# Two-layer hybrid encoder on one Trainium2 core: the modulation groups laid out anew, and the opening reordered

## The chip, the cores and the metric

The kernel runs on one core of one Trainium2 chip. The metric is the device time of one execution in microseconds (us), given as the median of several runs. Beside the runs there is one profiled execution, whose trace is the source of every duration below. Engines are named as the profile names them: PE is TensorE (matmuls; PEld its weight loads), DVE is VectorE, ACT is ScalarE, POOL is GpSimd, SP is SyncE, which here does nothing but issue DMAs.

## The reference, cut to what matters

A trunk of two layers over x of 1024 tokens by 1024 channels, all in float32, with one condition vector c. Each layer first turns c into six modulation vectors of 1024 numbers:

```
cond = silu(c)
for l in range(2):
    mod = cond @ w_mod[l] + b_mod[l]                  # 1 x 6144
    sh_a, sc_a, gt_a, sh_f, sc_f, gt_f = split(mod, 6)  # groups 0..5 of the layer
    h = rms_norm(x, g_attn[l]) * (1 + sc_a) + sh_a
    y = three_head_groups(h @ w_in[l])                # A, B and C, each with its own RMSNorm
    x = x + gt_a * (y @ w_o[l])
    h = rms_norm(x, g_ffn[l]) * (1 + sc_f) + sh_f
    gate, up = split(h @ w_gu[l], 2)                  # 1024 -> 2 x 2816
    x = x + gt_f * ((silu(gate) * up) @ w_down[l])    # 2816 -> 1024
return rms_norm(x, g_final)
```

A group is one of these six vectors of one layer, written (layer, group): (0,5) is gt_f of the first layer, (1,0) is sh_a of the second. Each needs a 1024 x 1024 block of w_mod, 4 MB, read once.

## The kernel before

x is kept transposed, channels on partitions, in eight chunks of 128 channels by 1024 tokens. A product of float32 accuracy is made of three fp32r matmuls: both operands are split into a high and a low part, and `mm3` adds high x high, low x high and high x low. ACT makes the high part (a cast), DVE or POOL the low one (a subtraction), into the `wpt` or `whl` buffers. Gate/up and down are Strassen-like: seven products instead of eight per block, with sums of weights made by DVE ahead.

**The stages and the engines' order.** In the opening, in the projections of the attention stage and in some others the instructions of an engine are pinned to the order of the source; elsewhere a scheduler in the compiler chooses the order by readiness. SP is pinned through gate/up and down. Whatever order results, each engine runs its own instructions one after the other, and SP its DMA issues.

**Opening.** Groups (0,0) and (0,1) come first, because h of layer 0 needs them. They are made in four pairs p, each of two channel chunks, from eight half loads `gm` of 1 MB: `gemv_half(i)` adds three weighted rows on DVE and lets PE add the rest into one row of PSUM; after the second half of a pair ACT copies the row to `gr`. `gemv_turn(p)` turns it into columns (four small PE transposes), `gemv_finish(p)` adds the bias on DVE, and `h_blocks(half, rows, ns)` makes the chunks ns of h for one half of the tokens: DVE scales (`nt`), ACT writes the high part `hh`, DVE the low part `hl`. `pair_done(p)` is the three of them in a row for the first half. `c_first(n)` then multiplies chunk n of that half with the weights of head group C, 12 matmuls into four banks `pssC`. The second half of x is squared (`x_square`), its norm is taken (`x_rms`, `spread` to rows) and it is transposed (`x_turn`) in between. After the opening, the loop over t goes on with `c_proj(4, 5)`, the same projection for the first two 128-token blocks of the second half, 48 matmuls over chunks 0 to 7.

**Modulation groups beside the matmuls.** The other groups run beside the main work, in the order of the list `todo`: (0,2) to (0,5), then (1,0) to (1,5). In each layer's attention stage `mod_one` takes 24 steps, three whole groups. In gate/up, `mod_stream(psl, shared, until)` is a generator: each `next` issues the load `wmt` of the next half row block (128 x 512, 256 KB) on SP and lets DVE add the block loaded before, weighted by c, to the accumulator `acc`; 16 such adds make a group. Then `mod_parts` and `mod_flush` split `acc` in two halves and sum each over the partitions: two matmuls on PE (`ps_mod`), and a cast, two multiplications or subtractions and a reduction on DVE. With all pauses a group takes 24 calls of `next`. The tiles of the loads come from a tag that `shared` names, `sq` with two buffers in gate/up.

**Gate/up.** There are 22 column blocks q. The first seven run two products early; then each q from 7 on runs seven products of 12 matmuls. For each product ACT copies (`take`) or DVE adds the result out of its bank before a later product may write it; the operands are prepared by `ahead.fill()` on ACT, DVE and POOL. The kernel before calls `next(mods_due)` after each product from q = 7 (`EARLY`) on, until (1,3): in layer 0 that is the four groups (0,5), (1,0), (1,1) and (1,2); in layer 1 the list is empty by then.

**Down.** 77 units u of 12 matmuls, prepared four units ahead: two high and two low parts per unit, `graw` loads of two units at a time from DRAM. After every eleventh unit DVE adds the banks into x (`residual`). After unit 54 of layer 0 the squares and h of layer 1 begin beside it, for which (1,0) and (1,1) must be there.

Of the kernel before, what the change touches and what calls it, by code (L numbers as in the profile page):

```python
# [19 lines left out]
P = 128  # L20
# [65 lines left out]
def trunk(ctx: ExitStack, tc, A, C, out):  # L86
# [266 lines left out]
    def mod_stream(psp, shared, until):  # L353


        pl, tag, bufs, width = shared
        acc = None
        while todo and todo[0] < until:
            l, g = todo[0]
            first = going["step"]  # L360
            if first == 0:
                going["acc"] = cp.tile([P, 1024], F32, name="acc", tag="acc")
            acc = going["acc"]
            halves = [(k, c0) for k in range(first, KC) for c0 in range(0, 1024, width)]
            loads = {}

            def load(i):
                k, c0 = halves[i]
                st = loads[i] = pl.tile([P, width], F32, name="wmt", tag=tag, bufs=bufs)
                g0 = g * 1024 + c0  # L370
                sp.dma_start(st, A["w_mod"][l, k * P : (k + 1) * P, g0 : g0 + width])

            if halves:
                load(0)
                yield
            for i, (k, c0) in enumerate(halves):
                if i + 1 < len(halves):
                    load(i + 1)
                mod_add(k, acc[:, c0 : c0 + width], loads.pop(i))
                yield  # L380
            going["step"] = KC
            mod_parts(slice(0, width), shared)
            while going["step"]:
                yield
                yield
                yield
                mod_flush(psp)
            yield
# [56 lines left out]
    def spread(r, j0, psp, tag="mm"):  # L445

        ps = psp.tile([P, 512], F32, name="ps_r", tag=tag)
        for j in range(4):
            pe.transpose(
                ps[:, j * P : (j + 1) * P], bc(r[:, j0 + j : j0 + j + 1], [P, P]), ident  # L450
            )
        return ps
# [116 lines left out]
    def x_rms(r):  # L569
        act.activation(r, r, AF.Sqrt, bias=epst, scale=1.0 / D)  # L570
        dve.reciprocal(r, r)

    def x_turn(half, xn, ns, engines):

        c = slice(half * H, (half + 1) * H)
        for n in ns:
            ps = psl.tile([P, 512], F32, name="ps_x", tag="mm")
            for i in range(4):
                pe.transpose(
                    ps[:, i * P : (i + 1) * P], xn[i][:, n * P : (n + 1) * P], ident  # L580
                )
            if engines[n % 2] is act:
                act.copy(xt[:, n, c], ps)
            else:
                dve.tensor_copy(xt[:, n, c], ps)
# [23 lines left out]
            rows = A["w_mod"][0, r0 : r0 + 4 * P, c0 : c0 + 2 * P]  # L609
            sp.dma_start(gm[:, :, g, :], rows.rearrange("(k p) n -> p k n", p=P))  # L610

    def gemv_half(i):
        p, s = i // 2, i % 2
        gm = gms.pop(i).rearrange("p k g n -> p k (g n)")
        if s == 0:
            gas[p] = stp.tile([P, 4 * P], F32, name="ga", tag="ga", bufs=2)
            gps[p] = psl.tile([P, 4 * P], F32, name="ps_mod", tag="mm")
        ga, row = gas[p], gps[p][0:1]
        for k in range(3):
            mod_add(4 * s + k, ga, gm[:, k])  # L620
        pe.matmul(row, condT[:, 4 * s + 3 : 4 * s + 4], gm[:, 3], start=(s == 0), stop=False)
        if s:
            pe.matmul(row, ones, ga, start=False, stop=True)
            gas[p] = stp.tile([1, 4 * P], F32, name="gr", tag="gr", bufs=1)
            act.copy(gas[p], row)

    def gemv_turn(p):

        ps = gps[p] = psl.tile([P, 4], F32, name="ps_m", tag="mm")
        row = gas.pop(p)  # L630
        for c in range(4):
            pe.transpose(ps[:, c : c + 1], row[:, c * P : (c + 1) * P], ident[0:1, 0:1])
# [35 lines left out]
            sp.dma_start(dst, v)  # L668
        wcs.append(st)

    def c_first(n):

        wh, wl = wC[n // 2]
        for t in range(T0):
            ts_ = slice(t * P, (t + 1) * P)
            mm3(
                pssC[t], hh[:, n, ts_], hl[:, n, ts_], wh[:, n % 2], wl[:, n % 2],
                n == 0, n == KC - 1,
            )
# [52 lines left out]
    def pair_done(p):  # L732
        gemv_turn(p)
        gemv_finish(p)
        if p == 0:
            keep_busy(8)
        h_blocks(0, rb, (2 * p, 2 * p + 1))
# [39 lines left out]
    pair_done(2)  # L777
    x_square(1, 1, xns[1][1], rxs[1])
    c_first(4)
    c_first(5)  # L780
    w_split()
    wab.append(w_ab(0, 1))
    spill(0)
    gemv_half(7)
    pair_done(3)
    for j in (2, 3):
        x_square(1, j, xns[1][j], rxs[1])
    x_rms(rxs[1])
    x_turn(1, xns[1], range(4), (act, act))
    c_first(6)  # L790
    x_turn(1, xns[1], range(4, KC), (act, act))
    c_first(7)
    spill(1)
    rows = spread(rxs[1], 0, psl)
    turn_vecs(1, v1)
    gm = stp.tile([P, 2048], F32, name="gm", tag="gm", bufs=3)
    first_t1 = c_norm_first(pssC[0], gm[:, 0:512], gm[:, 512:1024], gm[:, 1024:1032])
    for n in range(0, KC, 2):
        h_blocks(1, rows, (n, n + 1))
    sp.dma_start(sinkc, bc(A["sink_sw"].rearrange("l h -> (l h)")[None, :], [P, 12]))  # L800
    for l in range(2):
# [9 lines left out]
    for l in range(2):  # L811
# [1166 lines left out]
            shifted_sub(b21, b21, shift(2 * i + 1), t2)  # L1978
            h_split("t4", i, b21, dve)

        mods_due = mod_stream(psl, (ntp, "sq", 2, H), (1, 3))
        bs = []
        rows = None
        norm = rstd_rows(ssq, ntp, psl)
# [24 lines left out]
        for q in range(NF):  # L2009
            if q % 2 == 0:  # L2010
                gu_start(q // 2)
            if q == NF - 1:
                pin([act], True)
            if q < EARLY:
                up = q % 2
                e = sg[q // 2][0][:, 0:H]
                if up:
                    pool.tensor_tensor(out=e, in0=e, in1=quads[q]["11"], op=ALU.mult)
            for i, p in enumerate(PRODUCTS[2 if q < EARLY else 0 :]):
                gu_product(q, p, ahead.get())  # L2020
                if i == 1 and q < EARLY and not up:
                    act.activation(e, quads[q]["11"], AF.Silu)
                ahead.fill()
                g_step()
                if q >= EARLY:
                    next(mods_due, None)
        for _ in mods_due:
            pass
# [164 lines left out]
                yield  # L2193

        beside = iter(())
        for u in range(NU):
            i, t = divmod(u, NB)
            num, _, bank = DOWN[i]
            for what in due.get(u, ()):
                what()  # L2200
            ahead.fill(4)
            if u % 2 == 0 and (u + 6) // 2 <= (NU - 1) // 2:
                b_load((u + 6) // 2)
            for _ in range(3 if steps else 0):
                g_step()
            if u == 5:
                xt = blocks(xp)
            if t == 0 and num == 2:
                acc_b = [psl.tile([P, 512], F32, name="ps_d", tag="mm") for _ in range(4)]
            banks = acc_a if bank == "a" else acc_b  # L2210
            a, b = ahead.have.pop(0)
            for j in range(4):
                js = slice(j * P, (j + 1) * P)
                mm3(
                    banks[j], a[:, 0, js], a[:, 1, js], b[:, 0], b[:, 1],
                    num in (1, 2, 5) and t == 0, t == NB - 1, skip_group_check=True,
                )
            next(beside, None)
            if u >= NU - 2 and not last_layer:
                if u == NU - 2:  # L2220
                    wC = []
                wC.append(split_w(w_in_src(1, C_COLS, len(wC)), 2, eng=dve))
            if t < NB - 1:
                continue
            m, half = {
                1: (0, 0), 2: (0, 0), 6: (0, 1), 7: (1, 1), 4: (1, 0), 5: (1, 1), 3: (0, 1),
            }[num]
            for j in range(4):
                residual(banks[j], 2 * j + m, slice(half * H, half * H + H), 40)
            if num == 4:  # L2230
                close(w2_cm)
                close(w1_cm)
                if last_layer:
                    fn_cm, fnp = open_pool("fin", side="right")
                    gf = fnp.tile([P, D], F32, name="gf")
                    sp.dma_start(gf, bc(A["g_final"][None, :], [P, D]))
                else:
                    h_cm, hp = open_pool("h", side="right")
                    hh = hp.tile([P, KC, S], F32R, name="hh")
                    hl = hp.tile([P, KC, S], F32R, name="hl")  # L2240
                    cc_cm, ccp = open_pool("cc", side="right")
                    csts.clear()
                    g8 = gains_load(ccp, 1)
                    for n in range(KC):
                        at_unit(57 + 2 * n, lambda n=n: spill(0, [n]))
                beside = chain(early_half(), odd_squares())
# [111 lines left out]
```

## Time and profile before

| | |
|---|---|
| median of 3 runs | 2448.36 us (2446.49 to 2448.49) |
| the profiled execution: its own time | 2449.54 us |
| its span, first to last instruction | 2447.8 us |
| mean granted TensorE clock | 0.994 |
| instructions | 34293 |
| busy: PE, DVE, ACT, POOL | 97%, 74%, 50%, 31% of the span |
| DMA, mean over the span | 145 GB/s |

The page's busy shares are unions of an engine's instructions over the whole span. The view of windows gives the same for chosen stretches, with the granted clock (1.00 is full speed). The view of waits sums up how long an engine sat idle before a kind of instruction, and the instruction or DMA that ended it. In the views a line such as `ps_w<-ht3h,wpt` is an instruction that writes tile ps_w from ht3h and wpt; all lines are those of one helper (L49), so tiles tell them apart. `ps_w` are the banks of gate/up, `ps_d` of down, `ps_c` of the C projection.

### The profile page before, as it was taken

To read this page: it belongs to the slowest core of one execution; us is meant where nothing else is said; L and a number is where in the kernel's file an instruction comes from. 1 tells how busy PE (TensorE), PEld (TensorE's weight loads), DVE (VectorE), ACT (ScalarE), POOL (GpSimd) and SP (SyncE) were. 2 spreads that over 40 slices of the span, in tenths; PEclk is the share of its full clock that TensorE was granted. 3 is DMA by queue.
4 is the path that set the end of the run, shared out by engine and by line. 5 is a ranking of instruction groups with operands and counts; after the bars stand their busy time and mean duration, and the time that the engine had idled before them with its cause. 6 is when DMAs were issued, how large, how long until landed. Compare 5 with 4: busy or idle time off the path is not lost.

```text
span 2447.8 us, 34293 instructions
## 1 busy us (share of the span) xinstructions
PE 2385.3 (97%) x12005; PEld 1991.1 (81%) x12005; DVE 1819.0 (74%) x2968; ACT 1224.3 (50%) x2306; POOL 768.3 (31%) x783
## 2 busy tenths in 40 slices
PE   8999999999999999999999999999999999999998
PEld 5788899878788787788888889987887888888886
DVE  6757999987967777587677689998698555446865
ACT  3422888954543333334543158888454343334443
POOL 1531445620344343300036124464005434430001
PEclk9999999999999999999999999999999999999999
DMA  8468205154245453596434851241634432239743
GB/s 284 152 188 289 56 11 145 49 180 147 87 153 178 149 182 123 166 278 200 142 104 120 262 181 27 64 133 51 206 93 136 136 106 95 99 104 285 216 135 109
DMA packets 284181, 356.04 MB, mean 145 GB/s; under 512 B 32996, under 2 KB 201532, under 8 KB 284008
## 3 DMA queue, kind: packets, MB, share of 16 engines
q1 hardware_dynamic: 275512, 335.08, 44.1%
q10 hardware_dynamic: 6912, 12.59, 1.6%
q0 software_dynamic: 1584, 6.17, 0.7%
q8 instruction: 95, 1.56, 0.3%
q14 instruction: 78, 0.64, 0.1%
HBM read 269.62 MB, written 86.69 MB: 146 GB/s over the span
## 4 chain that ended last, share of the span: by engine, by line
PE 71%; DVE 11%; DMA 6%; issue 5%; ACT 4%; POOL 1%; SPq 1%; ACTq 0%; POOLq 0%; DVEq 0%
PE ps_w L49 28%; PE ps_d L49 10%; PE ps_o L49 7%; PE pv L49 6%; PE ps_ab L49 6%; PE T L49 4%; PE sC L49 3%; PE ps_c L49 2%; PE ps_v L49 2%; DMA wmt<-in_w_mod_dram 2%; DVE wpt L49 2%; DMA w<-in_w_down_dram 2%; ACT pr L49 1%; PE sA L49 1%; DVE w L49 1%
## 5 line engine op out<-in xcount | busy, mean ns | idle before, releaser
L49 PE MATMUL ps_d<-wpt 128*128 128x512 f32 x1848 | 425.2, 391 | 2.1 <-DVE wpt L49 0.9
L49 PEld LDWEIGHTS ps_d<-wpt 128*128 128x128 f32 x1848 | 345.6, 188 | 77.0 <-DVE wpt L49 3.1
L49 POOL TENSOR_SCALAR pr<-pr,rs 128x1024 f32<-128x1024 f32 (+4 forms) x252 | 206.9, 823 | 271.6 <-DVE rs L49 254.9
L49 POOL TENSOR_TENSOR sg<-sg,u 128x512 f32<-128x512 f32 x86 | 123.5, 1437 | 359.4 <-ACT sg L49 227.9
L49 PE MATMUL pv<-pt,vs 128*128 128x256 f32 x1216 | 202.1, 297 | 7.9 <-DVE rs L49 2.3
L49 DVE TENSOR_TENSOR pt<-T,pt 128x512 fp32r<-128x512 f32 x304 | 199.6, 681 | 11.4 <-ACT pt L49 9.9
L49 ACT CAST pt<-T 128x512 fp32r<-128x512 f32 x304 | 170.0, 586 | 43.8 <-PE T L49 41.9
L49 PE MATMUL T<-identr,pr 128*128 128x128 f32 x1288 | 187.1, 273 | 2.2 <-ACT rb L49 1.0
L49 ACT COPY u<-ps_w 128x512 f32<-128x512 f32 x128 | 75.2, 587 | 214.8 <-PE ps_w L49 214.8
L49 PEld LDWEIGHTS pv<-pt,vs 128*128 128x128 f32 x1216 | 161.3, 190 | 22.9 <-DVE y L49 7.6
L49 DVE TENSOR_TENSOR wpt<-w,wpt 128x512 fp32r<-128x512 f32 x154 | 111.6, 725 | 83.7 <-ACT wpt L49 83.7
L49 PEld LDWEIGHTS T<-identr,pr 128*128 128x128 f32 x1288 | 152.6, 140 | 21.9 <-issue 3.2
L49 POOL TENSOR_TENSOR wpt<-ws,wpt 128x512 fp32r<-128x512 f32 x80 | 112.0, 1401 | 182.8 <-ACT wpt L49 140.6
L49 DVE SCALAR_TENSOR_TENSOR acc<-wmt,condT,acc 128x512 f32<-128x512 f32 (+1 forms) x98 | 112.5, 1158 | 66.2 <-DMA wmt<-in_w_mod_dram 65.6
L49 ACT CAST wpt<-w 128x512 fp32r<-128x512 f32 x154 | 95.5, 620 | 131.3 <-PE ps_d L49 124.1
L49 ACT CAST wpt<-ws 128x512 fp32r<-128x512 f32 x176 | 107.9, 622 | 56.3 <-issue 22.5
L49 ACT CAST wpt<-graw 128x512 fp32r<-128x512 f32 x154 | 95.1, 617 | 78.0 <-DMA graw<-gpd 73.1
L49 DVE TENSOR_TENSOR wpt<-ws,wpt 128x512 fp32r<-128x512 f32 x96 | 83.0, 874 | 57.2 <-ACT wpt L49 57.1
L49 DVE TENSOR_REDUCE rs<-sC 128x1 f32<-128x1024 f32 x96 | 116.5, 1219 | 6.4 <-PE sC L49 6.0
L49 DVE TENSOR_TENSOR ws<-wr 128x512 f32<-128x512 f32 x88 | 82.2, 935 | 52.5 <-POOL wpt L49 49.5
L49 DVE TENSOR_TENSOR wpt<-graw,wpt 128x512 fp32r<-128x512 f32 x154 | 110.9, 720 | 12.5 <-ACT wpt L49 12.5
L49 PE MATMUL ps_w<-ht3h,wpt 128*128 128x512 f32 x352 | 112.0, 400 | 6.9 <-ACT sg L49 6.9
(288 smaller groups left out, 6030.5 us busy)
## 6 DMA issues: line engine op xcount, KB each, us to landing
wr<-in_w_gu_dram SPq DMA_DIRECT2D x92, 512.0 KB, 4.2
gpd<-sg SPq DMA_DIRECT2D x154, 256.0 KB, 4.5
graw<-gpd SPq DMA_DIRECT2D x76, 512.0 KB, 3.8
w<-in_w_down_dram SPq DMA_DIRECT2D x110, 256.0 KB, 5.1
wmt<-in_w_mod_dram SPq DMA_DIRECT2D x48, 512.0 KB, 6.6
qk<-qkd SPq DMA_DIRECT2D x44, 512.0 KB, 7.1
wst<-in_w_o_dram SPq DMA_DIRECT2D x32, 512.0 KB, 3.4
wmt<-in_w_mod_dram SPq DMA_DIRECT2D x64, 256.0 KB, 3.4
```

Of the source, the lines that this page charges most:

```text
L49: ins = op(*args, **kwargs)
```

## The change

Gate/up now calls `next(mods_due)` only after the products i = 0, 2, 4 and 6 of a q, and goes to (l + 1, 1 - l): in layer 0 the two groups (0,5) and (1,0), in layer 1 whatever is left. Down has a stream of its own, one call per unit from u = 37 on, with loads in the three `nt` buffers: in layer 0 that is (1,1), in layer 1 none. The attention stage of layer 1 with its 24 steps then makes (1,2), (1,3) and (1,4) where it made (1,3), (1,4) and (1,5), and gate/up of layer 1 makes (1,5). In all the same twelve groups are made.

In the opening, the last half of the gemv moves ahead of `c_first(5)`; the copy of its row becomes a function of its own (`gemv_row`), issued on ACT after the squares; `c_first(5)` is cut in two around `gemv_turn(3)`; the rows of the second half's norm are spread before `c_first(6)` instead of after `c_first(7)`, and chunks 0 to 3 of the second half's h are issued before `turn_vecs` and `c_norm_first` instead of after them.

```diff
-    def gemv_half(i):
+    def gemv_half(i, copy=True):
...
         if s:
             pe.matmul(row, ones, ga, start=False, stop=True)
-            gas[p] = stp.tile([1, 4 * P], F32, name="gr", tag="gr", bufs=1)
-            act.copy(gas[p], row)
+            if copy:
+                gemv_row(p)
+
+    def gemv_row(p):
+        row = gps[p][0:1]
+        gas[p] = stp.tile([1, 4 * P], F32, name="gr", tag="gr", bufs=1)
+        act.copy(gas[p], row)
...
-    def c_first(n):
+    def c_first(n, ts=None):
...
-        for t in range(T0):
+        for t in ts or range(T0):
...
     c_first(4)
-    c_first(5)
+    gemv_half(7, copy=False)
     w_split()
     wab.append(w_ab(0, 1))
     spill(0)
-    gemv_half(7)
-    pair_done(3)
     for j in (2, 3):
         x_square(1, j, xns[1][j], rxs[1])
     x_rms(rxs[1])
+    gemv_row(3)
+    c_first(5, (0, 1))
+    gemv_turn(3)
+    c_first(5, (2, 3))
+    gemv_finish(3)
+    h_blocks(0, rb, (6, 7))
     x_turn(1, xns[1], range(4), (act, act))
+    rows = spread(rxs[1], 0, psl)
     c_first(6)
+    h_blocks(1, rows, (0, 1))
     x_turn(1, xns[1], range(4, KC), (act, act))
     c_first(7)
     spill(1)
-    rows = spread(rxs[1], 0, psl)
+    h_blocks(1, rows, (2, 3))
     turn_vecs(1, v1)
...
     first_t1 = c_norm_first(pssC[0], gm[:, 0:512], gm[:, 512:1024], gm[:, 1024:1032])
-    for n in range(0, KC, 2):
+    for n in (4, 6):
         h_blocks(1, rows, (n, n + 1))
...
-        mods_due = mod_stream(psl, (ntp, "sq", 2, H), (1, 3))
+        mods_due = mod_stream(psl, (ntp, "sq", 2, H), (l + 1, 1 - l))
...
-                if q >= EARLY:
+                if q >= EARLY and i % 2 == 0:
                     next(mods_due, None)
...
         beside = iter(())
+        mods_due = mod_stream(psl, (ntp, "nt", 3, H), (l + 1, 2))
         for u in range(NU):
             i, t = divmod(u, NB)
+            if u > 36:
+                next(mods_due, None)
             num, _, bank = DOWN[i]
```

## The prediction

> **What bounds the kernel now.** I read the page's first part, then the waits of PE, then windows of the stages that the change touches, and only then the queues behind them.
>
> ```profile
> PE 2385.3 (97%) x12005; PEld 1991.1 (81%) x12005; DVE 1819.0 (74%) x2968; ACT 1224.3 (50%) x2306; POOL 768.3 (31%) x783
> ```
>
> PE works 97% of the span and the change takes no matmul away, so only two things can be won: time in which PE waits, and time in which it runs at a lower clock. The waits of PE, the three longest over the whole span:
>
> ```profile
> PE ps_w L49 <- ACT sg L49: 10.1, 6, 3.0
> PE ps_c L49 <- ACT hh L49: 9.0, 4, 4.4
> PE ps_w L49 <- ACT u L49: 4.2, 5, 1.9
> ```
>
> The first and third are gate/up: PE waits for ACT to copy a bank. The second is the opening. Both are stages that the change touches. Gate/up runs twice, and in layer 1 without modulation, which makes layer 1 the measure. Windows from q = 7 to the last product, layer 0 and layer 1, then down of layer 0 (columns: PE, PEld, DVE, ACT, POOL, clock, DMA share, GB/s):
>
> ```profile
> 730.40:1036.40 306.00, 296.37 (x1278) 242.12 (x1277) 220.44 (x271) 108.80 (x195) 126.30 (x87) 0.98 0.49 159
> 1931.20:2216.80 285.60, 285.60 (x1261) 236.59 (x1260) 137.36 (x170) 110.30 (x195) 117.23 (x87) 1.00 0.34 112
> 1036.40:1250.60 214.20, 212.58 (x938) 174.40 (x937) 161.17 (x250) 98.84 (x171) 13.32 (x10) 1.00 0.66 196
> ```
>
> The same 1260 matmuls take 306.0 us in layer 0 and 285.6 in layer 1, where PE never waits. A matmul is worth 285.6 / 1260 = 0.227 us, a product of 12 is 2.72 us. The 16 `ps_mod` matmuls of four groups are 3.6 us, so 20.4 - 3.6 = 16.8 us are lost in layer 0. PE's waits in that window are 9.6 of them:
>
> ```profile
> PE ps_w L49 <- ACT sg L49: 6.9, 4, 3.0
> PE ps_w L49 <- ACT u L49: 2.7, 3, 1.9
> ```
>
> The other 7.2 are matmuls at a lower clock behind the long waits. A wait and what follows it, twice:
>
> ```profile
> 919.90:922.90 3.00, 0.03 (x2) 0.00 (x1) 3.00 (x6) 1.16 (x3) 0.00 (x0) 0.85 0.11 37
> 922.90:929.30 6.40, 6.40 (x16) 5.06 (x17) 4.25 (x6) 2.29 (x5) 1.50 (x2) 0.54 0.01 1
> 852.80:855.10 2.30, 0.42 (x2) 0.00 (x1) 0.78 (x2) 2.09 (x5) 0.34 (x1) 1.00 0.08 19
> 855.10:859.00 3.90, 3.83 (x17) 3.15 (x18) 2.06 (x3) 1.82 (x5) 3.65 (x3) 1.00 0.97 329
> ```
>
> After 3.0 us without a matmul the clock is 0.54 for 6.4 us, which costs 6.4 x 0.46 = 2.9 us more; after 1.9 us nothing follows. [...]
>
> Why ACT is late in layer 0: not by its own work (108.8 against 110.3 us busy) but because its casts wait for DVE's sums, and DVE stands before a modulation add until its load has landed.
>
> ```profile
> DVE acc L49 <- DMA wmt<-in_w_mod_dram: 47.2, 25, 5.3
> SPq L49 <- DVE wpt L49: 73.5, 10, 16.7
> DMA to landing us min/median/max: 2.6/4.5/8.6
> 730.40:1036.40 306.00, 84.37 (x96) 0.98 0.49 159
> ```
>
> The rows: DVE's wait for `wmt`; SP's own wait for buffers, behind which the `wmt` loads queue; their time to landing; DVE's work on `acc` for four groups, 21.1 us each. A load is issued one step ahead, 2.72 us, and lands after 4.5. So DVE was taken for 220.4 + 47.2 = 268 of 306 us (87%) in layer 0 and 137.4 of 285.6 (48%) in layer 1.
>
> **The change, part by part: gate/up of layer 0.** Two groups go out. Those left are stepped after four products of seven: mostly 5.44 us apart, longer than the 4.5 of a landing, so most of DVE's waits go with it. DVE comes to 137.4 + 42.2 = 180 of 287 us, 63%. Bounds of what stays lost: nothing (layer 1's row) and 8.4 (two groups at 16.8 / 4 each). A straight line from 48% (0) to 87% (16.8) gives 6.5, but a queue that is late now and then holds PE only when the lateness outlasts the 2.72 us of the product in between; I take 2.
>
> **Gate/up of layer 1.** It receives (1,5) at the same pace: 137.4 + 21.1 = 158 us, 55%. Bounds 0 and 4.2; I take 1. The `ps_mod` matmuls only move from stage to stage: 0.9 us a group wherever it runs, nothing in the sum. The attention stage of layer 1 keeps its 24 steps, with other columns of w_mod: nothing.
>
> **Down of layer 0.** Here the new stream runs at one step per unit, 2.72 us, from u = 37 to 60. The window of these units, DVE's wait in it, and the landing of the `graw` loads of down:
>
> ```profile
> 1139.00:1202.00 63.00, 62.92 (x278) 51.87 (x277) 38.52 (x60) 29.45 (x52) 1.00 (x1) 1.00 0.45 134
> L49 DVE TENSOR_TENSOR wpt<-w,wpt 128x512 fp32r<-128x512 f32 x23 | 15.9, 691 | 23.5 <-ACT wpt L49 23.4
> DMA to landing us min/median/max: 3.4/3.8/11.0
> L49 DVE SCALAR_TENSOR_TENSOR acc<-wmt,condT,acc x56: 736/752/1850, 738.8 to 991.6; 128x512 f32<-128x512 f32 x56
> ```
>
> DVE has 24.5 us free of 63. Sixteen adds at 0.75 are 12 (the 1850 ns of the row are adds beside POOL, which is idle here), the two sums some 5: 55.5 of 63, 88%, before any wait for a load. On SP each second `wmt` stands behind the `graw` load of that pair of units, which waits for DVE's last subtraction on its buffer; so the chain subtraction, issue, landing, add, two subtractions must close once in two units. By rows: 0.3 + L + 0.7 + 2 x 0.69 = L + 2.4 us, against 5.44. With L = 4.2 (a `graw` landing and a little, the `wmt` being next behind it) that is 1.2 late per pair, 9 over eight pairs, of which the four units prepared ahead absorb some 6. Bounds: 0 (the scheduler is free to put the add behind the subtractions, DVE not being pinned there) and 9 (nothing absorbed); I take 3. If DVE is late, `residual` after unit 43 is late next, and unit 44 writes the same banks. The three `nt` buffers hold loads two steps old, and x is written to `nt` by `h_chunk` only from unit 65 on: no conflict, nothing. SP's `x_back` and `spill` behind the new loads have many units of lead: nothing, unless SP is late with `graw`, which is the chain just priced.
>
> **The opening.** The rows of PE there (the 49.71 and 74.79 are from the chain of waits: start, length), the windows around the longest pause and behind it:
>
> ```profile
> 57.74 0.40 PE L49 MATMUL ps_m<-identr,gr 1*128 1x1 f32 x4 [0.72 <-ACT gr L49]
> 60.92 0.51 PE L49 MATMUL ps_c<-whi,hl 128*128 128x512 f32 x1 [0.28 <-DVE hl L49]
> 68.97 0.23 PE L49 MATMUL pst<-identr,v 72*128 72x72 f32 x1
> 73.61 0.80 PE L49 MATMUL ps_c<-whi,hh 128*128 128x512 f32 x1 [4.41 <-ACT hh L49]
> 49.71 5.51 PE ps_c L49 x23
> 74.79 12.87 PE ps_c L49 x47
> 68.90:73.60 4.70, 0.30 (x4) 0.11 (x1) 3.82 (x9) 1.06 (x3) 1.37 (x2) 0.84 0.82 251
> 73.60:79.10 5.50, 5.11 (x12) 3.65 (x13) 5.36 (x7) 2.00 (x3) 3.33 (x3) 0.52 0.58 202
> 84.00:135.00 51.00, 51.00 (x268) 42.32 (x266) 43.85 (x67) 21.96 (x50) 34.90 (x29) 1.00 0.42 117
> ```
>
> PE is idle 4.4 us before `c_proj(4, 5)` because chunk 0 of the second half comes only after `turn_vecs` and DVE's five operations of `c_norm_first`; then it runs 5.5 us at 0.52, 5.5 x 0.48 = 2.6 lost, with short waits on `hl` 3.0. I laid the new order out by durations of DVE and ACT:
>
> ```profile
> L49 SPq DMA_DIRECT2D gm<-in_w_mod_dram x16: 367/530/1842, 3.0 to 34.8; - x16
> DMA to landing us min/median/max: 4.6/8.5/10.1
> 52.69 2.32 DVE L49 SCALAR_TENSOR_TENSOR ga<-gm,condT,ga 128x512 f32<-128x512 f32 x3
> 58.58 1.41 DVE L49 SCALAR_TENSOR_TENSOR nt<-xt,vecs,rb 128x512 f32<-128x512 f32 x2
> 59.36 1.38 ACT L49 ACTIVATE hh<-nt,vecs 128x512 fp32r<-128x512 f32 x2 [1.68 <-DVE nt L49]
> 60.12 1.41 DVE L49 SCALAR_TENSOR_TENSOR hl<-nt,vecs,hh 128x512 fp32r<-128x512 f32 x2
> 63.22 3.98 ACT L49 COPY xt<-ps_x 128x512 f32<-128x512 f32 x8
> 72.06 1.40 DVE L49 SCALAR_TENSOR_TENSOR nt<-xt,vecs,ps_r 128x512 f32<-128x512 f32 x2
> ```
>
> `c_first(4)`, the first half of the 24 matmuls to 55.2, ends at about 52.4 as before; the gemv's three adds on DVE, now ahead of the split of the weights, run from 50.3 to 52.7 (the last `gm` load is issued at 34.8 and lands within 10.1). The row is copied on ACT while six matmuls of `c_first(5)` run, and chunks 6 and 7 are made while PE transposes: the 0.7 before the turn, the 0.8 around 60.9 and half a microsecond of small gaps go, 2.0 together, and `turn_vecs` ends near 67.1 instead of 69.2. A pair of chunks takes 1.41 `nt` and 1.41 `hl` on DVE, with `hh` beside. Once the rows are spread (59.6), chunks 0 and 1 are done by 62.6, and 2 and 3, behind four copies of 0.5 on ACT, by 66.6: `c_proj(4, 5)` starts at once. From the end of `turn_vecs` to the next `nt` DVE needs 2.8 as before (69.2 to 72.06), so chunks 4 and 5 start at 69.9: the first is wanted at 67.1 + 24 x 0.227 = 72.5 and has its high part at 71.4; 6 is wanted at 75.2, at 74.3. It ends at 67.1 + 48 x 0.227 = 78.0 instead of 87.7: 9.5 us = 2.0 + 4.5 (idle) + 3.0 (clock). Behind it PE has not waited once from 84 to 135, with DVE 86% busy; DVE is earlier by about 9 and keeps up. The rows `ps_r` hold one more bank for longer, three stay for `x_turn`: some 0.1. On SP `spill` and `w_ab` only start with the work they follow: nothing. Bounds 6 (the two last pairs each late by a wait) and 10.
>
> **Sum**, against the profiled execution: 2449.5 - 9.5 - 16.8 + 2 + 1 + 3 = 2429.2. The median of the runs is 1.2 under the profiled one: 2428.
>
> **The rivals.** (a) The loss belongs to each group, not to its pace: 4.2 us a group wherever it is put, because each group's sums and adds come in clusters. For it: the seven waits of gate/up lie over all four groups. Against: loads that come in time. Then only the opening is won: 2448.4 - 9.5 = 2439. (b) Down: the chain above is late by 9, and one wait at unit 44 reaches 3 us, so the clock falls for 2.9: 8 to 9 in place of 3, 2434. For it: 88%; against: PE waits there now for 0.7 us only, twice. (c) The opening's gain is half given back because DVE, 86% busy behind it, is what really sets the pace: 2433. (d) The other side: the landing of `wmt` in down decides. Without down 23.3 us are won (9.5 + 16.8 - 3); the loss there is 8 x (L + 2.4 - 5.44) - 6, which reaches 23.3 at L = 6.7 us. The longest landing of this tile is 8.6, which gives 38 us and 2463. Against: `graw`, in the same stage, lands in 3.8 by the median. (e) Nothing is won: the waits move elsewhere one for one, and `hh` is late at its later chunks as it was at the first: 2448.
>
> ```profile
> PE ps_d L49 <- ACT wpt L49: 0.7, 1, 0.7
> PE ps_d L49 <- DVE wpt L49: 0.7, 1, 0.7
> ```
>
> (The waits of PE in down of layer 0, for b.)
>
> **How the numbers follow.** The forecast 0.54, (a) 0.12, (b) 0.13, (c) 0.12, (d) 0.05, (e) 0.04. The forecast's own range is 2423 to 2434: all of the 26.3 won and a little from the opening's upper bound, or 6 more lost. The range to 2440 takes in (a), (b) and (c), and leaves out (d) and (e); below, 2420. Faster by over 0.2%, 4.9 us, is the forecast with (a), (b), (c): 0.91; within 0.2%, about what a measurement of this kernel can tell from no change: 0.04; slower: 0.05.
>
> **What would show it.** In the profile after: the wait of 4.41 on `hh` gone and the clock 1.00 where it was 0.52; `c_proj(4, 5)` ending near 78; gate/up of layer 0 from q = 7 in 288 to 291 us and of layer 1 in 286 to 289; DVE's wait for `wmt` there well under 47.2 us; in down of layer 0 PE's waits on `wpt` or on `residual` by a few us around units 44 to 58. I am wrong if `c_first(5)` waits for the gemv row, if clocks under 1.00 stay in gate/up, or if down's 214 us grow by more than 9.

## The result, and the profile after

| | before | changed |
|---|---|---|
| median of 4 runs each, us | 2447.43 (2445.47 to 2448.49) | 2433.04 (2431.26 to 2435.46) |
| ratio, 95% interval | | 0.9943 (0.9926 to 0.9960) |
| the profiled execution, its own time | 2449.54 | 2432.24 |
| its span; mean granted clock | 2447.8; 0.994 | 2430.5; 0.996 |

The changed kernel is 14.4 us faster by the medians, 17.3 by the two profiled executions. The forecast was 2428 with a range of 2420 to 2440. The first line of the page after, and from the waits of PE over the whole span the three kinds that the prediction began with, beside two new ones (us in total, times, the longest):

```profile
PE 2378.9 (98%) x12005; PEld 1986.7 (82%) x12005; DVE 1829.2 (75%) x2968; ACT 1225.1 (50%) x2306; POOL 764.7 (31%) x783
PE ps_c L49 <- ACT hh L49: 4.6, 3, 2.0
PE ps_w L49 <- ACT sg L49: 3.9, 4, 1.6
PE ps_d L49 <- DVE xb L49: 2.5, 1, 2.5
PE ps_w L49 <- ACT u L49: 1.5, 2, 0.7
PE ps_ab L49 <- ACT whi L49: 1.7, 1, 1.7
```

The long wait on `hh` is gone (9.0 to 4.6 in all, the longest 2.0 instead of 4.4), gate/up's waits on `sg` and `u` fell from 14.3 to 5.4, and two are new: one on `xb` in down, which the prediction had named, and one on `whi`, which it had not. Where the time went is read by stage, from the start of the first matmul of each in the two traces (down of layer 0 ends with the start of its last matmul). The `ps_mod` matmuls, 0.9 us a group, only move; the last column is without them.

| stage, us | before | after | difference | forecast, without `ps_mod` | measured, without `ps_mod` |
|---|---|---|---|---|---|
| start to gate/up of layer 0 | 592.5 | 585.5 | -7.0 | -9.5 | -7.0 |
| gate/up, layer 0, from q = 7 | 306.0 | 289.0 | -17.0 | -14.8 | -15.2 |
| down, layer 0 | 213.9 | 215.8 | +1.9 | +3 | +1.0 |
| end of down to gate/up of layer 1 | 541.7 | 543.6 | +1.9 | 0 | +1.9 |
| gate/up, layer 1, from q = 7 | 285.6 | 287.0 | +1.4 | +1 | +0.5 |
| the rest | | | +1.5 | 0 | +1.5 |

The rest is down of layer 1 (+0.8), where nothing changed, the early products of gate/up (+0.4) and the tail (+0.3); over the runs below down of layer 1 took 215.2 to 217.4 us in whatever kernel. The windows of gate/up of both layers and of down, in the columns of the prediction:

```profile
723.80:1012.80 289.00, 288.24 (x1270) 237.85 (x1269) 190.14 (x220) 109.66 (x195) 123.20 (x87) 1.00 0.43 140
1911.40:2198.40 287.00, 286.94 (x1266) 237.14 (x1265) 163.51 (x195) 109.89 (x195) 120.50 (x87) 1.00 0.39 125
1012.80:1228.60 215.80, 212.51 (x941) 174.98 (x940) 175.93 (x276) 99.22 (x171) 13.56 (x10) 1.00 0.70 214
```

With 285.6 us for the products and 1.8 for two groups' sums, layer 0 keeps a loss of 289.0 - 285.6 - 1.8 = 1.6 us of its 16.8; layer 1 has 0.5. In layer 0's window PE waits 0.8 us in all, and yet DVE waits for its loads nearly as long as before:

```profile
PE ps_w L49 <- ACT sg L49: 0.8, 2, 0.4
DVE acc L49 <- DMA wmt<-in_w_mod_dram: 44.7, 21, 5.2
SPq L49 <- DVE wpt L49: 117.0, 16, 16.5
DMA to landing us min/median/max: 2.6/4.6/5.6
```

44.7 us of wait for 32 adds, where it was 47.2 for 64, and SP still held by `wpt` ahead of the `wmt` loads. So the gain is there and the way to it that the prediction gave ("loads that come in time") is not.

In the opening, `c_proj(4, 5)` starts at once behind the transpose of `turn_vecs` and the clock stays up; short waits are left, one of them at a new place (rows of PE; one window of it; the two subtractions on DVE that make `hl` of chunks 4 to 7):

```profile
67.73 0.23 PE L49 MATMUL pst<-identr,v 72*128 72x72 f32 x1
67.76 0.47 PE L49 MATMUL ps_c<-whi,hh 128*128 128x512 f32 x1
74.73 0.50 PE L49 MATMUL ps_c<-whi,hl 128*128 128x512 f32 x1 [0.18 <-DVE hl L49]
79.56 0.39 PE L49 MATMUL ps_ab<-hh,whi 128*128 128x512 f32 x1
74.70:80.00 5.30, 5.27 (x22) 4.12 (x23) 4.76 (x9) 3.21 (x6) 1.13 (x1) 1.00 0.39 111
125.52 0.34 PE L49 MATMUL pk<-identr,qn 128*128 128x128 f32 x2 [0.64 <-DVE qn L49]
72.35 2.33 DVE L49 SCALAR_TENSOR_TENSOR hl<-nt,vecs,hh 128x512 fp32r<-128x512 f32 x2
76.13 1.41 DVE L49 SCALAR_TENSOR_TENSOR hl<-nt,vecs,hh 128x512 fp32r<-128x512 f32 x2
```

### The profile page after: what moved, and what is told of

It reads as the page before. It is cut to its first block, busy times and chain, and to the rows that moved or that the text cites. A ratio compares the mean times of both kernels' runs of the same rounds, so it can differ in the third digit from the quotient of the medians.

```text
span 2430.5 us, 34269 instructions
## 1 busy us (share of the span) xinstructions
PE 2378.9 (98%) x12005; PEld 1986.7 (82%) x12005; DVE 1829.2 (75%) x2968; ACT 1225.1 (50%) x2306; POOL 764.7 (31%) x783
## 5 line engine op out<-in xcount | busy, mean ns | idle before, releaser
L49 DVE TENSOR_TENSOR pt<-T,pt 128x512 fp32r<-128x512 f32 x304 | 199.3, 680 | 11.2 <-ACT pt L49 9.6
L49 DVE SCALAR_TENSOR_TENSOR acc<-wmt,condT,acc 128x512 f32<-128x512 f32 (+1 forms) x98 | 105.7, 1086 | 80.1 <-DMA wmt<-in_w_mod_dram 79.9
L49 DVE TENSOR_TENSOR wpt<-ws,wpt 128x512 fp32r<-128x512 f32 x96 | 88.2, 927 | 53.0 <-ACT wpt L49 52.8
L49 DVE TENSOR_TENSOR wlo<-wst,whi 128x1024 fp32r<-128x1024 f32 x72 | 94.4, 1312 | 33.7 <-ACT whi L49 30.0
```

The source lines that it names most:

```text
L49: ins = op(*args, **kwargs)
```

## The experiments

Two questions: what of the change brings what, and why gate/up loses less although its loads are as late. Then two for what the change cost: the wait in down, and the one at the start of layer 1.

**Each part alone.** `e1_open` is the kernel before with the new opening, `e2_mods` the kernel before with the new places of the groups.

> The opening alone; the modulation groups stay as in the kernel before. If the changed kernel's ledger is right, PE is 7 us ahead of the kernel before when gate/up of layer 0 begins, gate/up of layer 0 still loses its 16.8 us (306 us from q = 7), and the whole is 7 us faster: about 2440. If instead the opening's gain comes only together with the new layout, or is given back in the attention stage, the whole is within 3 us of before.

> The new layout of the groups alone; the opening as before. Theory: gate/up of layer 0 from q = 7 takes 289 us instead of 306, down of layer 0 1.8 more, gate/up of layer 1 1.4 more, and the first projections of layer 1 some 2 to 4 more: in all 10 us faster, about 2437. Rival: the loss of 4 us at the start of layer 1 belongs to the opening's shift and is absent here: 14 us faster, 2433.

Measured: `e1_open` 2440.26 us, ratio 0.9959 (0.9943 to 0.9975); `e2_mods` 2439.01, ratio 0.9960 (0.9948 to 0.9972). Each is worth about 10 us alone, within some 4 either way, and together they are worth 14 (10 to 18); the intervals are too wide to say whether the two add up. By stages, `e1_open` reaches gate/up at 588.2 and has 303.3 us there; `e2_mods` reaches it at 592.8 and has 288.9. So gate/up's gain comes with the groups alone. The one trace of `e1_open` has 4.3 us of its gain ahead of gate/up, where the changed kernel has 7.0, and 2.7 in gate/up itself, where nothing was changed: with the same stream as before PE lost 303.3 - 285.6 - 3.6 = 14.1 us there and not 16.8. The start of gate/up varies too, by up to 3.4 us between traces of one order: over all of them it is at 592.5 to 594.8 in the five with the old opening (or its late chunks) and at 584.8 to 588.2 in the nine with the new one. The means, 593.5 and 586.0, make the opening worth 7.4 us. ACT's wait of 4.5 us at the start of layer 1, of which more below, is there in `e2_mods` and not in `e1_open`: it came with the groups and not with the opening's shift.

**Which part of the opening.** `e6_late_h` is the changed kernel with chunks 0 to 3 of the second half's h made late again.

```diff
     c_first(6)
-    h_blocks(1, rows, (0, 1))
...
     spill(1)
-    h_blocks(1, rows, (2, 3))
...
-    for n in (4, 6):
+    for n in range(0, KC, 2):
         h_blocks(1, rows, (n, n + 1))
```

> The changed kernel with chunks 0 to 3 of the second half's h issued after the C norm again, as in the kernel before; the rest of the new opening stays. If these chunks are what removed the wait of 4.4 us and the low clock behind it, both are back (4 us idle before the projection of the second half, clock near 0.5 behind it) and PE begins gate/up of layer 0 some 6 to 7 us later than in the changed kernel, near 592. If the earlier gemv alone did it, it begins within 1 us of 585.5.

```profile
PE ps_c L49 <- ACT hh L49: 4.4, 1, 4.4
```

The wait is back in full (waits of PE between 50 and 150 us of `e6_late_h`), the clock is low behind it (0.69 from 72.6 to 78.0), gate/up starts at 592.9, and the run took 2438.42 where the kernel before took 2442.98 on that chip, one run each. Without the early chunks nothing of the opening's gain is left that shows: moving the gemv and cutting `c_first(5)` in two bring none by themselves. Whether the early chunks would bring it all without these two was not tested.

**Pace, waits or work in gate/up.** Three kernels, one run each: 2439.68, 2440.86 and 2438.97 us, where the kernel before took 2442.98 on that chip. `e3_pace` is the changed kernel with a step after every product instead of every other. `e4_nowait` is the kernel before with adds that read a tile that is always there. `e5_nowork` is the kernel before with adds of 8 columns instead of 512, behind the same loads.

```diff
e3_pace, against the changed kernel
-                if q >= EARLY and i % 2 == 0:
+                if q >= EARLY:
e4_nowait, against the kernel before
-                mod_add(k, acc[:, c0 : c0 + width], loads.pop(i))
+                loads.pop(i)
+                mod_add(
+                    k, acc[:, c0 : c0 + width].rearrange("p (a b) -> p a b", a=4),
+                    bc(ident[:, None, :], [P, 4, P]),
+                )
e5_nowork, against the kernel before
+                if k == 0:
+                    mod_add(k, acc[:, c0 : c0 + width], loads.pop(i))
+                else:
+                    mod_add(k, acc[:, c0 : c0 + 8], loads.pop(i)[:, 0:8])
```

> The changed kernel, but with a step of the modulation after every product of gate/up again, for the same two groups in layer 0 and one in layer 1. If the pace is what costs, gate/up of layer 0 from q = 7 loses some 8 us (two groups at 4.2) instead of 1.6 and takes 295 to 296 us, and layer 1 some 4 instead of 0.5: 290 to 291. If only the number of groups in the stage counts, they stay at 289 and 287.

> The kernel before with the adds of the stream in gate/up reading a resident tile instead of the loaded one; the loads are still issued and land unread. It leaves out the sums of these four groups, so its output is not the reference's. DVE's work is the same, its waits for the loads (47 us) are gone. If these waits hold up the casts and so PE, gate/up of layer 0 from q = 7 falls from 306 to 289 to 293 us. If DVE's own work does it, it stays over 300.

> The kernel before with each add of the stream cut to 8 of 512 columns (from the second row block on), which leaves most of these four groups' sums out: DVE still waits for each load, but has some 50 us less to do. If the waits are what holds PE, gate/up of layer 0 from q = 7 stays over 300 us; if DVE's work is, it falls to 289 to 293.

The windows of gate/up of layer 0 from q = 7, in this order, the waits of PE there in `e3_pace`, and DVE's wait for loads in `e3_pace` and in `e5_nowork`:

```profile
724.20:1020.00 295.80, 290.39 (x1270) 238.91 (x1268) 178.56 (x220) 109.47 (x195) 122.67 (x87) 0.99 0.42 136
732.70:1029.30 296.60, 291.83 (x1278) 238.96 (x1277) 222.53 (x268) 109.17 (x195) 129.08 (x87) 1.00 0.51 164
732.20:1027.30 295.10, 292.26 (x1277) 240.38 (x1276) 191.62 (x271) 109.87 (x195) 122.53 (x87) 0.99 0.51 165
PE ps_w L49 <- ACT sg L49: 2.8, 2, 2.0
PE ps_w L49 <- ACT u L49: 2.6, 2, 1.9
DVE acc L49 <- DMA wmt<-in_w_mod_dram: 27.3, 16, 5.2
DVE acc L49 <- DMA wmt<-in_w_mod_dram: 66.5, 30, 5.3
```

| kernel | groups, pace | DVE busy + waiting for `wmt`, us | lost by PE, us |
|---|---|---|---|
| before | 4, each product | 220.4 + 47.2 of 306.0 | 16.8 |
| `e1_open` | 4, each product | 222.4 + 44.0 of 303.3 | 14.1 |
| `e4_nowait` | 4, each product | 222.5 + 9.3 of 296.6 | 296.6 - 285.6 - 3.6 = 7.4 |
| `e5_nowork` | 4, each product | 191.6 + 66.5 of 295.1 | 5.9 |
| `e3_pace` | 2, each product | 178.6 + 27.3 of 295.8 | 295.8 - 285.6 - 1.8 = 8.4 |
| changed | 2, every other | 190.1 + 44.7 of 289.0 | 1.6 |

`e3_pace` against the changed kernel settles the main point: the same two groups lose 8.4 us at every product and 1.6 at every other one. The loss follows the pace; the number of groups alone does not set it. That 8.4 is just twice 4.2, a quarter of the 16.8 before, is chance, for the groups do not lose alike. How far PE had fallen behind after so many products from q = 7 on, against the same products in layer 1 of the kernel before, with 0.227 us taken off for each `ps_mod` matmul:

| us behind after | 32 products | 56 | 80 | 104 |
|---|---|---|---|---|
| before | 1.9 | 5.3 | 11.5 | 16.8 |
| `e1_open` | 1.4 | 4.4 | 9.1 | 14.1 |
| `e3_pace` | 2.2 | 8.4 | 8.4 | 8.4 |
| changed | 0.7 | 0.8 | 1.5 | 1.6 |
| `e3_pace`, layer 1 | 0.9 | 0.9 | 0.9 | 0.9 |
| changed, layer 1 | 0.4 | 0.5 | 0.5 | 0.5 |

At every product a group takes 24 products, and these columns lie behind the first, second, third and fourth. The first group of a stream costs 0.9 to 2.2 us at that pace, the later ones 3.0 to 6.2; why they cost more was not tested. This answers the one expectation of the pace that failed: the single group of layer 1, at every product in `e3_pace`, lost 287.4 - 285.6 - 0.9 = 0.9 us and not some 4, and a first group is all it is.

Waits for loads are no measure of it: the slower pace has the longer ones (44.7 against 27.3), because DVE, less pressed, comes to its add earlier and stands there. `e4_nowait` and `e5_nowork` say that neither half of a step is the cause alone. In `e4_nowait`, with 9.3 of the 47.2 us of waits left (at the sums instead of the adds), 7.4 of the 16.8 stay; there 6 of the 64 adds ran before the window, for they had no load to wait for. In `e5_nowork`, with adds of 0.23 us instead of 0.75, 28.8 us less work on DVE and more waiting, 66.5, 5.9 stay. Either half cut down takes more than half of the loss away. That fits steps that must be done with, wait and work together, before the next is due; how many 2.72-us products a step may take before PE feels it was not measured, and DVE's busy and waiting share does not tell it: at 81% the changed kernel loses 1.6 us, at 70% of the window `e3_pace` loses 8.4, its four waits between 767 and 851 us, while its groups run.

**The wait in down.** In the changed kernel PE waits at unit 44 for `residual` to free the banks. DVE's rows ahead of it, PE's, and windows over the wait and behind it:

```profile
1130.77 0.75 DVE L49 SCALAR_TENSOR_TENSOR acc<-wmt,condT,acc 128x512 f32<-128x512 f32 x1 [1.21 <-DMA wmt<-in_w_mod_dram]
1132.75 0.75 DVE L49 SCALAR_TENSOR_TENSOR acc<-wmt,condT,acc 128x512 f32<-128x512 f32 x1 [1.23 <-DMA wmt<-in_w_mod_dram]
1134.62 2.72 DVE L49 SCALAR_TENSOR_TENSOR xb<-ps_d,vecs,xb 128x512 f32<-128x512 f32 x4
1135.51 5.69 PE L49 MATMUL ps_d<-wpt 128*128 128x512 f32 x24 [2.51 <-DVE xb L49]
1133.00:1135.50 2.50, 0.00 (x1) 0.02 (x1) 2.50 (x5) 1.14 (x2) 0.00 (x0) 1.00 1.00 346
1135.50:1141.00 5.50, 5.49 (x24) 4.60 (x25) 5.50 (x9) 1.14 (x2) 0.00 (x0) 1.00 0.22 51
```

The four residual adds could begin when unit 43 ended, near 1133.0, and begin at 1134.62, because two modulation adds ahead of them waited 2.4 us for their loads and pushed the subtractions back. Four kernels on this: `e7_lead` issues the loads in down two steps ahead, `e11_down_nowait` lets the adds there read a tile that is always there, `e12_skip` and `e13_early` leave units 42 to 44 out (both with the tile moved that the next part is about).

```diff
e7_lead
-    def mod_stream(psp, shared, until):
+    def mod_stream(psp, shared, until, lead=1):
...
-                load(0)
...
-                if i + 1 < len(halves):
-                    load(i + 1)
+                if i + lead < len(halves):
+                    load(i + lead)
e12_skip
-            if u > 36:
+            if u > 36 and u not in (42, 43, 44):
e13_early
-            if u > 36:
+            if u > 33 and u not in (42, 43, 44):
```

> The changed kernel with the loads of the stream in down issued two steps ahead instead of one (three buffers are there already). If PE's wait of 2.5 us on DVE's residual at unit 44 comes from DVE standing before adds whose load has not landed (8.5 us of waits between units 37 and 61), these waits fall under 2 us, the wait at unit 44 falls under 0.5 us, and the whole gains 2 us. If it is DVE's work itself, the wait at unit 44 stays over 2 us.

> The changed kernel, with the modulation adds of the stream in down of layer 0 reading a tile that is always there; the loads are still issued but nothing reads them (the sums of that modulation group are left out). If TensorE's 2.5 us wait at unit 44 comes from DVE's waits for the loads (8.5 us in 8 between 1112 and 1180 us): those are 0, the wait at unit 44 is under 0.5 us and down takes 213.5 to 214.5 us instead of 215.8. If it comes from the adds' own time on DVE: the wait stays at 2 us or more and down at 215 to 216.

> The kernel with the moved scratch tile, and the stream in down leaves out units 42, 43 and 44, in which the boundary between two halves of the tokens lies (its 24 steps then end three units later). If the price at unit 44 is DVE's steps ahead of it, whether by waiting or by work: the wait there is under 0.5 us instead of 2.5, down takes 213.5 to 215 us, and the time is 1 to 3 us under the kernel with the moved tile alone, so 2427 to 2431. If it is there whatever DVE does (a bank that is free late anyway): the wait stays at 2 us or more and the time is that of the moved tile alone. Under either, the adds skipped here delay nothing later as long as the group is done before the last unit.

> The kernel with the moved scratch tile, and the stream in down of layer 0 starts three units earlier (34 instead of 37) and leaves out units 42, 43 and 44, so that its last load is issued when it was in the changed kernel, ahead of layer 1's small loads. If the two prices of down are places (the steps just ahead of the boundary at unit 44, and a last load behind the small loads, which landed in 11.2 us where the stream had moved three units later): the wait at unit 44 is under 0.5 us, TensorE's wait for the sums' transposition is under 0.3 us, down takes 213.5 to 214.8 us, and the time is 2428 to 2431, 2 to 5 under the changed kernel's 2433. Rival, the steps cost the same wherever they stand: another boundary or unit loses 1.5 to 2.5 us, down stays at 215.5 to 217, and the time is that of the moved tile alone, 2431 to 2433.

DVE's wait for `wmt` between 1112 and 1180 us is 8.5 us in 8 in the changed kernel. The rows that answer, of `e7_lead` (DVE, then PE in down), `e11_down_nowait` (DVE, then PE in down) and `e12_skip` (SP's issues, DVE, PE, and the landing of its `wmt` loads):

```profile
DVE acc L49 <- DMA wmt<-in_w_mod_dram: 6.8, 6, 1.8
PE ps_d L49 <- DVE xb L49: 1.8, 2, 1.6
```

```profile
DVE wpt L49 <- ACT wpt L49: 23.2, 17, 1.4
PE ps_d L49 <- ACT wpt L49: 0.7, 1, 0.7
```

```profile
1162.96 0.43 SPq L49 DMA_DIRECT2D g<-in_gq_ax_dram  x1
1164.03 1.90 SPq L49 DMA_DIRECT2D cst<-const_rope_dram  x4
1165.97 0.43 SPq L49 DMA_DIRECT2D wmt<-in_w_mod_dram  x1
1177.21 0.75 DVE L49 SCALAR_TENSOR_TENSOR acc<-wmt,condT,acc 128x512 f32<-128x512 f32 x1 [6.55 <-DMA wmt<-in_w_mod_dram]
1178.62 0.50 PE L49 MATMUL ps_mod<-accl,onesr 128*128 128x512 f32 x1 [1.48 <-DVE accl L49]
DMA to landing us min/median/max: 3.8/4.3/11.2
```

| kernel | start of unit 43 to that of 44, us (2.96 in the kernel before) | down, us (213.9 before) | all runs: median, ratio |
|---|---|---|---|
| changed | 5.39 | 215.8 | 2433.04, 0.9943 (0.9926 to 0.9960) |
| `e7_lead` | 4.48 | 215.9 | 2433.16, 0.9933 (0.9913 to 0.9952) |
| `e11_down_nowait` | 2.96 | 213.7 | 2434.85, one run |
| `e12_skip` | 3.02 | 217.1 | 2432.96, 0.9939 (0.9923 to 0.9956) |
| `e13_early` | 3.36 | 214.8 | 2430.77, 0.9925 (0.9911 to 0.9939) |

The cause is DVE's waits for loads: with the same adds and all but 1.5 us of the waits gone (`e11_down_nowait`) PE's wait is gone and down takes 213.7 us, though its one total has a wait of PE of 3.0 us in gate/up of layer 0, where it does not differ from the changed kernel. One step more of lead removes little of them (8.5 to 6.8), and the 4.48 of `e7_lead` lies among the 3.98 to 5.39 that other kernels with the changed kernel's down show, so it settles nothing. `e12_skip` freed unit 44 and moved the price: three units later, the last load was issued behind layer 1's first small ones (`g`, `cst`) and landed in 11.2 us, DVE stood 6.55 us before it, and PE waited 1.48 for the sums. My expectation that later steps would delay nothing was wrong. `e13_early` keeps both places free: no load took over 6.1 us and PE's wait for the residual is 0.7 us in all, though DVE waits for its loads as long as before, 8.7 us in 9. It is where these waits fall that costs. Down is 1.0 us shorter, at the edge of what was expected.

**The start of layer 1.** This is the loss that no step of the prediction had. ACT's cast of the first weights there, in the kernel before and in the changed one, PE behind it in the changed one, and what POOL does up to it:

```profile
1281.53 1.05 ACT L49 CAST whi<-wst 128x1024 fp32r<-128x1024 f32 x1 [0.68 <-POOL hl L49]
```

```profile
1263.55 1.04 ACT L49 CAST whi<-wst 128x1024 fp32r<-128x1024 f32 x1 [4.46 <-POOL ct L49]
1264.65 0.49 PE L49 MATMUL ps_ab<-hh,whi 128*128 128x512 f32 x1 [1.69 <-ACT whi L49]
1266.01 0.50 PE L49 MATMUL ps_ab<-hh,wlo 128*128 128x512 f32 x1 [0.86 <-DVE wlo L49]
1260.85 2.67 POOL L49 TENSOR_TENSOR ct<-sq,cst 128x512 f32<-128x512 f32 x3 [1.14 <-DVE sq L49]
1266.50:1269.00 2.50, 2.50 (x9) 1.92 (x8) 2.06 (x5) 0.78 (x2) 0.35 (x1) 0.64 0.83 250
1269.00:1270.50 1.50, 1.50 (x5) 1.19 (x4) 0.73 (x2) 1.01 (x3) 1.50 (x2) 0.50 0.11 33
```

ACT stands 4.46 us until POOL has read `sq`, a scratch tile that `whi` has nothing to do with, and starts 0.03 after POOL's last read ends (1260.85 + 2.67 = 1263.52). The reason is the place of that tile: the tags of the scratch pool of down get their memory in the order of their first use. In the kernel before `sq` comes first and `nt` behind it. The new stream uses `nt` at unit 37, ahead of `sq`, so the two change places: in the built programs `sq` moves from bytes 98176 to 102272 of each partition to 104320 to 108416, the very bytes of layer 1's first `whi`. `e8_swap` exchanged the two buffers of `sq`, which changed no instruction's place: the slots are given at first use, not by name. So it tested nothing and is a repeat of the changed kernel. `e10_place` takes the tile that POOL reads from the tag `nt`.

```diff
e8_swap
-            *(ntp.tile([P, H], F32, name="sq", tag="sq", bufs=2) for _ in range(2)),
+            *[ntp.tile([P, H], F32, name="sq", tag="sq", bufs=2) for _ in range(2)][::-1],
e10_place
-            *(ntp.tile([P, H], F32, name="sq", tag="sq", bufs=2) for _ in range(2)),
+            ntp.tile([P, H], F32, name="sq", tag="sq", bufs=2),
+            ntp.tile([P, H], F32, name="cq", tag="nt", bufs=3),
```

> The changed kernel with the two scratch tiles of the first C norm of layer 1 taken in the other order, so that each lies where the other lay; the work is the same. If the 4.5 us that ACT waits on POOL before its first cast of layer 1's weights come from where these tiles lie in memory (the cast's target lies on the one that POOL still reads), the wait falls to under 1 us as in the kernel before, PE's waits on that cast and its low part (1.7 and 0.9 us, and the lower clock behind them) go, and the whole gains 2 to 4 us. If it is DVE or POOL being late after down, the wait stays.

> The changed kernel with one of the two scratch tiles of layer 1's first normalization (the one that POOL squares and reads) taken from the tag of the modulation loads, so that the first weight cast of layer 1's attention no longer writes over it. Place: ACT's wait of 4.46 us on POOL at that cast falls to under 1 us, TensorE's waits there (1.7 on whi, 0.9 on wlo) go, the stretch from the end of down of layer 0 to the first product of gate/up of layer 1 goes from 543.6 us to 540 to 542, and the time is 2 to 4 us under the changed kernel's 2433. Rival, lateness (POOL and DVE are still at the work that the late residual of down moved back): the wait goes to another tile and stays at 3 us or more, the stretch stays at 543 to 545, the time at 2432 to 2435.

ACT's cast and POOL's reads in `e10_place`, and the one wait of PE that is left there:

```profile
1261.99 1.03 ACT L49 CAST whi<-wst 128x1024 fp32r<-128x1024 f32 x1
1263.92 3.60 POOL L49 TENSOR_TENSOR ct<-cq,cst 128x512 f32<-128x512 f32 x3 [1.21 <-DVE cq L49]
1272.65 0.50 PE L49 MATMUL ps_ab<-hh,whi 128*128 128x512 f32 x1 [0.45 <-DVE cq L49]
```

The cast now comes ahead of POOL's reads, and the stretch from the end of down to gate/up of layer 1 takes 541.3 us; it is 541.3 in `e12_skip` and `e13_early` too, and 543.3 to 545.2 in the seven kernels with the changed layout and the tile in its old place. So the place of the tile is shown to be the cause. The rival, that POOL and DVE are late after down, is not borne out: in `e11_down_nowait`, where down lost nothing, ACT waits for POOL at that cast with the same 4.5 us. The times: `e8_swap` 2436.18 (ratio 0.9944, 0.9925 to 0.9963), `e10_place` 2431.1 (0.9931, 0.9916 to 0.9947). 2.3 us by the trace; by the intervals of the runs `e10_place` and the changed kernel can't be told apart.

`e13_early`, the moved tile and the stream of down in its best place, has the lowest median: 2430.77 us over five runs (2428.10 to 2431.15), 0.9925 of the kernel before (0.9911 to 0.9939). Its interval still overlaps the changed kernel's.

## Why the prediction was right, and where it was not

It was right on the total, and the two terms that carried it are the ones that the runs show: gate/up of layer 0 gave 15.2 us, where 14.8 were forecast, and the opening 7.0, where 9.5 were; the other stages took 4.9 back, where 4 were forecast. Point by point:

- **Gate/up, that the pace frees PE: right in size, wrong in mechanism.** I argued that loads 5.44 us apart come in time and that DVE's waits go. They did not: 44.7 of 47.2 us stayed. What went is the crowding of steps, each a wait and an add: two groups lose 8.4 us at each product, 1.6 at every other one (`e3_pace`). The 2 us that I left as lost were 1.6, the 1 in layer 1 was 0.5. That 15.2 came so near to 14.8 is in part luck: measured from `e1_open`, where the old stream lost 14.1, it would have been 12.5. And the 7.2 us of loss beside the waits were not all a lower clock: the window behind the other long wait (below, of the kernel before) gives 5.1 x 0.33 = 1.7, with the 2.9 behind the first 4.6 in all. The straight line from DVE's share, which I set aside, would have been worse: at DVE's 81%, busy and waiting, it gives some 14 us. Rival (a), a fixed 4.2 us a group, is excluded by the same pair of kernels.

```profile
1006.90:1012.00 5.10, 5.06 (x15) 4.02 (x16) 3.02 (x5) 1.87 (x4) 1.28 (x1) 0.67 0.01 3
```

- **The opening: right in kind, 2.5 us too much** (2.1 by the means of all executions). The wait of 4.41 and the low clock went as said, and `e6_late_h` shows that the early chunks did it. `c_proj(4, 5)` was to start at 67.1 and end at 78.0; it started at 67.8, which was not followed up, and ended at 79.6. The term that was mis-sized is the chunks behind it: I let chunks 4 to 7 arrive just in time, and `hl` of the first pair took 2.33 us instead of 1.41 on DVE, so each of the next pairs was a little late, 0.9 us together. Another 1.0 is lost around 125.5, where PE waits for `qn` (0.64 as one wait): I had written that PE had not waited once there and that DVE keeps up, and DVE did not. That is rival (c) at work at its place, with 1.0 and not with half the gain.
- **Down: right in kind, 2 us too much.** "`residual` after unit 43 is late next, and unit 44 writes the same banks" is what the trace shows, with 2.5 us, and DVE's wait for loads is its cause (`e11_down_nowait`). I took 3; down lost 1.0 beside its own `ps_mod`. The landing that I took as 4.2 us was 4.2 by the median and 5.5 at most, so rival (d), which needed 6.7, had no ground here; `e12_skip` shows that it was not idle, with 11.2 us for one load three units later. Rival (b) named the place and asked too much: its fall of the clock after the wait did not come (1.00 in the window behind the 2.5 us). By the last section the length of a pause does not tell that, so this was in part luck.
- **The start of layer 1: missed.** "The three `nt` buffers hold loads two steps old ... no conflict, nothing" looked at who uses the buffers of `nt` and not at where a new first use puts the other tags. It cost 1.9 us, and 2.3 came back when one tile was moved.

## What to carry to other kernels

Here side work beside a saturated engine was priced by its pace more than by its amount: spread the steps out, so that the engine that does them can finish each, wait and work, before the next is due, and do not read the waits of that engine as the loss. When a change gives a scratch tag an earlier first use, the tags behind it move, and a tile of another stage may come to lie on one that is still read: look in the changed profile for a wait on a tile that the waiting instruction has no use for. A step moved away from one collision is to be followed to where it lands; the same three units later, a load met the next stage's small ones and took 11.2 us.

## What the runs showed of the hardware

- In these traces the length of a pause of PE does not tell whether the clock falls behind it. Two pauses and the windows behind them, of `e5_nowork` and of `e11_down_nowait`:

```profile
997.90 0.74 PE L49 MATMUL ps_w<-ht3h,wpt 128*128 128x512 f32 x2 [1.88 <-ACT sg L49]
999.30:1002.70 3.40, 3.40 (x10) 2.64 (x9) 1.59 (x2) 0.46 (x2) 0.44 (x1) 0.51 0.00 0
989.37 0.73 PE L49 MATMUL ps_w<-ht3h,wpt 128*128 128x512 f32 x2 [3.00 <-ACT sg L49]
989.40:993.00 3.60, 3.60 (x16) 2.99 (x17) 0.88 (x1) 1.97 (x5) 1.30 (x1) 1.00 0.02 5
```

1.88 us were followed by 0.51, and 3.00 us by 1.00. In the changed kernel the 2.5 us in down were followed by 1.00, and two pauses of 1.69 and 0.86 us, with half a microsecond of work between them, at the start of layer 1 by 0.64 and 0.50.

- Between 60 and 2410 us the clock falls four times in the kernel before: it is at 0.50 from 72.1 to 78.9 us, 0.50 from 922.0 to 928.8, 0.51 from 1007.3 to 1010.7 and 0.50 from 1843.6 to 1847.0; in the changed kernel it falls twice, to 0.50 from 1267.2 to 1270.6 and from 1823.6 to 1827.0. In the 3.4 us ahead of these falls PE was idle for 2.9, 2.1, 2.8 and 2.0 us, and for 1.7 and 2.1. But in the 3.4 us from 1132.6 on, which hold the pause in down of the changed kernel, it was idle for 2.5, and the clock stayed at 1.00. What sorts them was not shown.
- The same pair of subtractions on DVE (`hl`) took 1.41 us at 76.1 and 2.33 at 72.4 of the changed kernel's execution. POOL was multiplying (`ct`) from 71.0 to 74.1, beside the slow pair; that it was the cause was not tested.
